# The last block of frames: scaled into DRAM, loaded in quarters, and turned by VectorE

## The chip, the cores and the metric

The kernel runs on one core of a Trainium2 chip. The metric is the device time of one execution in microseconds (us). Before the change the median of three runs is 937.81 us (937.69 to 938.49).

## The reference

One layer of a streaming encoder, in fp32, for 2048 prompt frames and 32 sample frames of 1024 columns:

- `hn = rmsnorm(h) * g_mix`, then one projection `hn @ w_in` to six parts of 512 columns (hA, bA, cA, zA, vB, zB).
- Mixer A: `u = cA * hA`, a causal convolution of width 3 over the frames, `yA = bA * conv * silu(zA)`. Mixer B: trailing means over 2, 4, 8 or 16 frames minus the frame, a 128x128 map per group of columns, `yB = that * silu(zB)`.
- `h += concat(yA, yB) @ w_out`, then `h += (p @ w_ple) * sigmoid(rmsnorm(h) @ w_gate)`, and a last rmsnorm.

The change concerns the first line alone: `hn` for the last 416 frames, and how its columns get onto the partitions, where the projection needs them.

## The kernel before, in words

The 2080 frames are five blocks of 416 (`NB`), in groups [0, 1], [2, 3] and [4]. A product is done in three passes of a rounded high part and the rest (`split`, lines 76 to 79: ACT casts, DVE subtracts). For a group of two blocks, seven products of halves replace eight, with sums of frames and of weights as operands.

The projection goes by units: four per group (j = 0 to 3), each with six kinds of weights for 128 columns. A unit of the first or second group runs three pairs of kinds (`pair`, line 847): seven products of halves a pair, and a `yield` between them. After each of these 24 steps of a unit `aside()` is called (line 949), which advances preparation of later frames: `at_pace(steps, num, den)` runs `num` steps of a generator per `den` calls. In the second group, from j = 1 on, the generator is `last_block` (line 1043), one step per three calls (line 1101).

`last_block` prepares block 4: three chunks of 128 prompt frames and one of 32 sample frames, c = 0 to 3. Per chunk, x is loaded (frames on partitions), ACT takes the sum of squares (line 88), POOL the scale factor (lines 69 and 73), DVE scales it by that and by g_mix (`normal`, line 406). Then in two halves of 512 columns: four 128x128 transposes on PE into PSUM (`turn`, line 413, against `ident`), and `to_memory` (line 480), which splits from PSUM into a staged tile and stores it to the DRAM tensor `b_d` from POOL's queue. The chunk takes three steps: scaling, half, half.

The third group frees the ring of frames (`xin`, five buffers of 128x1024 floats, which also holds the staged tiles), reads `b_d` into `hn[4]` (line 1077), and puts a pool `ya` into the freed memory, whose first loads (y, x and rows of w_out, lines 314, 327, 319) are issued as soon as it is free. A unit of this group is six plain products of 24 matmuls. After the projection come the products with w_out, the embedding, and the gate, whose frames are partly turned on PE (`turned`) and partly by loads in quarters and DVE's 32x32 blocks (`turned_here`, line 1297).

The order on each engine is set by a list scheduler: it orders what is ready by its own estimate of times, earlier traced first. `keep_in_program_order(ins)` pins an instruction behind the one traced before it on its engine (later ones may still be put ahead); every engine and every DMA queue then runs in that order. SP's queue carries the raw weights (line 511), the frames (line 392) and the stores of y_d (line 705).

Of the kernel before, what the change touches and what calls it, by code (L numbers as in the profile page):

```python
# [9 lines left out]
F32 = mybir.dt.float32  # L10
F32R = mybir.dt.float32r
AF = mybir.ActivationFunctionType
ALU = mybir.AluOpType
PSUM = bass.MemoryType.PSUM

P = 128
D = 1024
KC = D // P
# [6 lines left out]
NB = 416  # L25
# [3 lines left out]
KH = KC // 2  # L29
# [5 lines left out]
def trunk(ctx, tc, x_p, x_s, c_conv, c_pool, p_p, p_s, g_mix, w_in, conv_w, conv_b, pool_w,  # L35
          pool_scale, w_out, g_ple, w_gate, w_ple, g_fin, y_p, y_s, sc_p, sp_p, sc_s, sp_s):
    nc = tc.nc
# [38 lines left out]
    def split(hi, lo, src, eng=nc.vector):  # L76
        ins = nc.scalar.copy(hi, src)  # L77
        eng.tensor_tensor(lo, src, hi.bitcast(F32), op=ALU.subtract)
        return ins
# [3 lines left out]
    g_bc = const.tile([P, D], F32, name="g_bc")  # L83
# [20 lines left out]
    def embed(todo, wp, ring, queue=nc.sync):  # L104

        got = {}

        def prep(c):
            if c in got or c >= len(todo):
                return
            i = todo[c]
            r, n = tiles[i]
            if c % 4 == 0:
                pt = ring("p", i)
                m = min(4, len(todo) - c)
                full = [j for j in todo[c:c + m] if j < NT - 1]
                if full:  # L120
                    nc.sync.dma_start(pt.rearrange("p (a d) -> p a d", a=4)[:, :len(full)],
                                      p_p[r:r + len(full) * P].rearrange("(a p) d -> p a d", p=P))
                if len(full) < m:
                    nc.sync.dma_start(pt[:DEC, len(full) * PLE:(len(full) + 1) * PLE], p_s)
                got["p"] = pt
            pt = got["p"][:, (c % 4) * PLE:(c % 4 + 1) * PLE]
            pps = ring("pps", i)
            ptp = tbank(f"ptp_{i}")
            for k in range(2):
                nc.tensor.transpose(ptp[:, k * P:k * P + n], pt[:n, k * P:(k + 1) * P], ident[:n, :n])  # L130
            v = ptp.rearrange("p (k t) -> p k t", k=4)[:, :2, :n]
            split(pps[:, 0, :, :n], pps[:, 1, :, :n], v)
            got[c] = pps

        def run(c, last=False):
            i = todo[c]
            r, n = tiles[i]
            prep(c)
            prep(c + 1)
            prep(c + 2)  # L140
            pps = got[c]
            o = ring("out", i)
            for nh in range(2):
                cs = slice(nh * NH, nh * NH + NH)
                ps = bank(f"e_{i}_{nh}")
                embed_product(ps, pps, wp, cs, n)
                (nc.vector.tensor_copy if last and nh else nc.scalar.copy)(o[:n, cs], ps[:n])
            (nc.gpsimd if last else queue).dma_start(e_d[r:r + n], o[:n])

        return prep, run  # L150
# [141 lines left out]
    def slot(name):  # L292
        return acts[0].tile([P, SLOT], F32R, tag="hn", name=name)
# [13 lines left out]
    def ring4(t, name):  # L307
        return t.tile([P, D], F32, tag="t", name=name)
# [15 lines left out]
    def load_rows(pool, name, i, pr, sa=None):  # L324
        r, n = tiles[i]
        t = ring4(pool, f"{name}_{i}")
        nc.sync.dma_start(t[:n], pr[r:r + n] if sa is None else rows_of(pr, sa, r, n))
        return t

    with ExitStack() as s1:  # L330
# [5 lines left out]
        xin = frames_in.enter_context(tc.tile_pool(name="xin", bufs=5, side="right"))  # L336
# [11 lines left out]
        def put(piece, src):  # L348

            return split(piece[:, :, 0], piece[:, :, 1], src)  # L350
# [45 lines left out]
        def x_stat(x, later=False):  # L396

            t, n, name = x
            return t, n, sumsq(t, n, name, later=later)
# [4 lines left out]
        def normal(x):  # L404
            xt, n, r = x
            nc.vector.scalar_tensor_tensor(xt[:n], xt[:n], r[:n], g_bc[:n], op0=ALU.mult, op1=ALU.mult)  # L406

        def turn(x, half, name, get=tbank, later=False):
            xt, n, _ = x
            pt = get(name)  # L410
            for k in range(KH):
                kk = half * KH + k
                ins = nc.tensor.transpose(pt[:, k * P:k * P + n], xt[:n, kk * P:(kk + 1) * P], ident[:n, :n])
                if later:
                    tc.keep_in_program_order(ins)
            return pt.rearrange("p (k t) -> p k t", k=KH)[:, :, :n]
# [58 lines left out]
        b_d = tc.dram_tile([P, KC, 2, NB], F32, name="b_d")  # L475

        def staged(name):
            return xin.tile([P, KH, 2, P], F32R, tag="t", name=name)

        def to_memory(mem, name, src, at, n, t=None, later=False):  # L480
            t = t or staged(name)[:, :, :, :n]
            ins = put(t, src)
            if later:
                tc.keep_in_program_order(ins)
            nc.gpsimd.dma_start(mem[:, :, :, at:at + n], t.bitcast(F32))
# [98 lines left out]
        for c, x in enumerate([*ahead0, short0]):  # L584
            normal(x)
            n = P if c < 3 else DEC
# [433 lines left out]
        def load_ahead(g, c):  # L1020
            ahead[g, c] = columns_in(g, c) if g == 1 else [x_load(f"4_{c}", [x_rows(4, c)])]
# [21 lines left out]
        def last_block():  # L1043

            load_ahead(2, 0)
            for c in range(4):
                x = x_stat(ahead.pop((2, c))[0], True)
                if c < 3:
                    load_ahead(2, c + 1)
                normal(x)  # L1050
                yield
                for half in range(2):
                    pt = turn(x, half, f"pt4_{c}_{half}", later=True)
                    to_memory(b_d[:, half * KH:half * KH + KH], f"b_4_{c}_{half}", pt, c * P, x[1])
                    yield

        def at_pace(steps, num, den):

# [11 lines left out]
        for gi, tbs in enumerate(GROUPS):  # L1070
            if gi == 2:

                frames_in.close()
                t = slot("hn_4")
# [13 lines left out]
            for j in range(4):  # L1088
                unit = gi * 4 + j
                u = Unit(gi, tbs, j)  # L1090
                if unit == 0:
                    u.plain()
                    B0["T4"] = piece_of(seventh("B0_T4"), 0)
                    nc.sync.dma_start(B0["T4"].bitcast(F32), p_d["T4"])
                    p_d["T4"] = tc.dram_tile([P, KH, 2, NB], F32, name="p_dT4b")
                    aside = at_pace(next_columns(3, 0, 1, 2), 39, 62)
                elif gi == 0:
                    u.seven(B, aside)
                elif gi == 1:
                    if j == 1:  # L1100
                        aside = at_pace(last_block(), 1, 3)
                    u.seven(B, aside, j == 0)
                else:
                    u.plain()
                if gi == 2:
                    early_sums(j)
# [5 lines left out]
    with ExitStack() as s2:  # L1112
# [111 lines left out]
        for i in range(0, NT - 1, 2):  # L1224
            with tc.issue_after(loaded[-1].ins):
                x = [load_rows(xh, "x", i + b, x_p) for b in range(2)] if i else [first_x, second_x]
# [4 lines left out]
            if last:  # L1231
                n = tiles[NT - 1][1]
# [6 lines left out]
            if last:  # L1239
                x = load_rows(xh, "x", NT - 1, x_p, x_s)  # L1240
# [27 lines left out]
        _, run = embed(rest_e, wp, ring)  # L1268
# [195 lines left out]
        n = tiles[NT - 1][1]  # L1464
# [5 lines left out]
        h, e = (load_rows(*a) for a in ((xh, "h", NT - 1, h_d), (ya, "e", NT - 1, e_d)))  # L1470
        plain("gl", A, W, n, *short_ops(h, e, n))
        done_g(NT - 1, h)
        for i in range(0, NT - 3, 2):
            A = S.pop(i)
            h = [load_rows(xh, "h", i + b, h_d) for b in range(2)]
# [34 lines left out]
```

## Time and profile before

| | before |
|---|---|
| median of three runs | 937.81 us |
| the profiled execution | 940.76 us, its span 939.0 us |
| TensorE (PE) busy | 918.3 us, 98% |
| PE's weight loads busy | 829.4 us, 88% |
| VectorE (DVE) busy | 727.4 us, 77% |
| ScalarE (ACT) busy | 482.2 us, 51% |
| GpSimd (POOL) busy | 129.3 us, 14% |
| granted TensorE clock, mean | 0.992 |
| DMA | 182.97 MB, 195 GB/s |

The span runs from the first to the last instruction of the profiled execution; the 1.76 us around it are in its time. A group of instructions is shown with its line, engine, operation and its tiles, out<-in; "<-" behind an idle time names what ended it. Matmuls overlap one another in the records, so their cost is read from one start to the next. Numbers of tiles are left out in part, so tiles of several units share a name.

### The profile page before, as it was taken

How to read it: one execution, taken by the hardware profiler on the slowest of the kernel's cores; microseconds unless marked ns; L12 is line 12 of the kernel's file. 1: busy time of each engine (PE TensorE's matmuls, PEld its weight loads, DVE VectorE, ACT ScalarE, POOL GpSimd, SP SyncE). 2: the span in 40 equal slices, each digit the busy share in tenths (PEclk: the TensorE clock that was granted, in tenths of full speed). 3: DMA queues.
4: the chain of work that ended last, by engine and by line, in shares of the span. 5: the costliest groups of instructions: out<-in, count | busy, mean ns of one | idle time of the engine just before them, and what ended most of it. 6: DMA issues, size and time to landing. Idle time of an engine off the chain costs nothing.

```text
span 939.0 us, 13008 instructions
## 1 busy us (share of the span) xinstructions
PE 918.3 (98%) x4567; PEld 829.4 (88%) x4567; DVE 727.4 (77%) x1230; ACT 482.2 (51%) x894; POOL 129.3 (14%) x244
## 2 busy tenths in 40 slices
PE   6999999999999999999999999999999999999996
PEld 5899998999999999999999987888877868888885
DVE  6796898899588978685777589665554797888985
ACT  5653555464445554443444456334334875555663
POOL 2110232212000110000000010111211001211123
PEclk8999999999999999999999999999999999999998
DMA  8335556769955645427655359866785884566553
GB/s 240 85 121 175 154 146 203 222 174 297 417 167 139 180 142 166 129 71 272 195 167 175 128 187 289 270 181 183 218 244 171 318 264 129 206 220 244 183 207 113
DMA packets 133215, 182.97 MB, mean 195 GB/s; under 512 B 11164, under 2 KB 105116, under 8 KB 131869
## 3 DMA queue, kind: packets, MB, share of 16 engines
q1 hardware_dynamic: 117165, 131.70, 45.0%
q0 software_dynamic: 13248, 44.93, 14.6%
q10 hardware_dynamic: 2736, 5.51, 1.8%
q8 instruction: 36, 0.59, 0.3%
q14 instruction: 30, 0.25, 0.1%
HBM read 127.23 MB, written 54.86 MB: 194 GB/s over the span
## 4 chain that ended last, share of the span: by engine, by line
PE 79%; ACT 1%; DMA 1%; DVE 1%; POOL 0%; issue 0%; POOLq 0%; SPq 0%; ACTq 0%
PE x_o L167 9%; PE x_g L167 9%; PE x_zab L561 5%; PE x_ch L561 5%; PE x_zbv L561 5%; PE e L102 5%; PE z_g L167 5%; PE z_o L167 4%; PE z_ch L561 3%; PE z_zab L561 3%; PE z_zbv L561 2%; PE y_g L167 2%; PE y_o L167 2%; PE b L561 2%; PE za L561 2%; PE c L561 2%
## 5 line engine op out<-in xcount | busy, mean ns | idle before, releaser
L77 ACT CAST y_S<-y_fS 128x512 fp32r<-128x512 f32 x32 | 19.5, 621 | 43.1 <-PE x_o L167 19.4
L102 PE MATMUL e<-wq,pps 128*128 128x512 f32 (+1 forms) x156 | 38.8, 399 | 0.2 <-ACT pps L77 0.2
L406 DVE SCALAR_TENSOR_TENSOR xt<-xt,rstd_x,g_bc 128x1024 f32<-128x1024 f32 (+2 forms) x18 | 23.1, 1282 | 17.7 <-POOL rstd_x L73 17.5
L167 PE MATMUL x_g<-wg_b,g_S 128*128 128x512 f32 x128 | 35.9, 390 | 0.0
L167 PE MATMUL x_o<-wo_b,y_S 128*128 128x512 f32 x128 | 35.8, 391 | 0.0
L561 PE MATMUL x_zab<-B,w_zab_S 128*128 128x416 f32 x168 | 34.3, 352 | 0.5 <-ACT V L859 0.5
L561 PE MATMUL x_ch<-B,w_ch_S 128*128 128x416 f32 x168 | 34.6, 352 | 0.0
L561 PE MATMUL x_zbv<-B,w_zbv_S 128*128 128x416 f32 x168 | 34.4, 353 | 0.0
L561 PE MATMUL z_ch<-B,w_ch_S 128*128 128x416 f32 x168 | 34.1, 351 | 0.0
L561 PE MATMUL z_zbv<-B,w_zbv_S 128*128 128x416 f32 x168 | 34.1, 351 | 0.0
L561 PE MATMUL z_zab<-B,w_zab_S 128*128 128x416 f32 x168 | 34.0, 351 | 0.0
L102 PEld LDWEIGHTS e<-wq,pps 128*128 128x128 f32 (+1 forms) x156 | 27.4, 182 | 6.9 <-ACT pps L77 0.5
L561 PEld LDWEIGHTS x_zab<-B,w_zab_S 128*128 128x128 f32 x168 | 31.3, 188 | 1.1 <-ACT V L859 0.8
L561 PEld LDWEIGHTS x_zbv<-B,w_zbv_S 128*128 128x128 f32 x168 | 31.1, 188 | 0.8 <-ACT zs L859 0.4
L561 PEld LDWEIGHTS x_ch<-B,w_ch_S 128*128 128x128 f32 x168 | 31.2, 188 | 0.6 <-ACT c_s L859 0.3
L561 PEld LDWEIGHTS z_zab<-B,w_zab_S 128*128 128x128 f32 x168 | 31.4, 188 | 0.3
L561 PEld LDWEIGHTS z_ch<-B,w_ch_S 128*128 128x128 f32 x168 | 31.3, 188 | 0.4
L561 PEld LDWEIGHTS z_zbv<-B,w_zbv_S 128*128 128x128 f32 x168 | 31.3, 188 | 0.3
L69 POOL TENSOR_SCALAR ms_f<-ssq_f 128x1 f32<-128x1 f32 (+1 forms) x15 | 8.8, 588 | 160.7 <-ACT junk L88 160.7
L77 ACT CAST y<-y 128x512 fp32r<-128x512 f32 x24 | 14.8, 618 | 29.6 <-PE x_o L167 13.7
L1332 DVE SCALAR_TENSOR_TENSOR h<-h,rstd_f,g_bc 128x1024 f32<-128x1024 f32 (+1 forms) x15 | 19.3, 1284 | 12.7 <-POOL rstd_f L73 12.7
L167 PEld LDWEIGHTS x_o<-wo_b,y_S 128*128 128x128 f32 x128 | 24.0, 188 | 5.1 <-ACT c_o L1136 0.3
(571 smaller groups left out, 2670.4 us busy)
## 6 DMA issues: line engine op xcount, KB each, us to landing
y<-y_d SPq DMA_DIRECT2D x16, 512.0 KB, 12.8
x<-in_x_prompt_dram SPq DMA_DIRECT2D x16, 512.0 KB, 9.0
h_d<-x SPq DMA_DIRECT2D x16, 512.0 KB, 4.8
h<-h_d SPq DMA_DIRECT2D x16, 512.0 KB, 4.1
xt<-in_x_prompt_dram SPq DMA_DIRECT2D x15, 512.0 KB, 6.4
e<-e_d SPq DMA_DIRECT2D x15, 512.0 KB, 6.3
out_dram<-h POOLq DMA_DIRECT2D x14, 512.0 KB, 3.0
p_dT<-T POOLq DMA_DIRECT2D x12, 512.0 KB, 5.4
```

The costliest lines, as they stand in the source:

```text
L69: nc.gpsimd.tensor_scalar(ms[:n], ssq[:n], scalar1=1.0 / D, scalar2=EPS, op0=ALU.mult, op1=ALU.add)
L77: ins = nc.scalar.copy(hi, src)
L102: nc.tensor.matmul(ps[:n], pps[:, a, k, :n], wp[k][b][:, cs], start=k + q == 0, stop=k == 1 and q == 2)
L167: nc.tensor.matmul(ps[:n], lhs[:, k, a, :n], w[b][:, k], start=start and k + q == 0, stop=k == KH - 1 and q == 2, skip_group_check=True)
L406: nc.vector.scalar_tensor_tensor(xt[:n], xt[:n], r[:n], g_bc[:n], op0=ALU.mult, op1=ALU.mult)
L561: nc.tensor.matmul(ps[:, :NB], lhs[:, k, x], b[:, k, y], start=start and k + q == 0, stop=stop and k == KH - 1 and q == 2, skip_group_chec ...
L1332: nc.vector.scalar_tensor_tensor(h[:n], h[:n], rf[:n], g_bc[:n], op0=ALU.mult, op1=ALU.mult)
```

## The change

`last_block` no longer turns the chunks on PE.

- Scaling (`scaled_to_memory`): DVE scales in four pieces of 256 columns. Piece q takes from each of the eight runs of 128 columns (k) the 32 columns q*32 to q*32+31, and writes them side by side, in another tile of the ring `xin`. POOL's queue stores the tile to a new DRAM tensor `xs_d`. The pieces are pinned in DVE's order.
- Loading (`from_memory`): SP's queue loads quarter q of `xs_d` onto partitions 32q to 32q+31, with the chunk's groups of 32 frames beside each other.
- Turning (`turned_in_place`): one DVE instruction turns every 32x32 block in place, pinned in DVE's order. That leaves column on the partition and frame along it, as the transposes did.
- `halves_to_memory` splits the halves from SBUF and stores them to `b_d` as before. The ACT cast is pinned, as it was.

The generator has 18 steps where it had 12. Chunk c is scaled in one step, the chunk before it is turned, split and stored in the next two, and then chunk c is loaded; the first chunk is loaded in the step after its scaling. The pace stays at a step per three calls.

```diff
             load_ahead(2, 0)
-            for c in range(4):
+            back = {}
+
+            def scale(c):
                 x = x_stat(ahead.pop((2, c))[0], True)
                 if c < 3:
                     load_ahead(2, c + 1)
-                normal(x)
+                scaled_to_memory(x, c * P)
+                return x[1]
+
+            def halves_to_memory(c, n):
+                u = turned_in_place(back.pop(c))
+                for half in range(2):
+                    t = staged(f"b_4_{c}_{half}")[:, :, :, :n]
+                    v = lambda h: t[:, :, h].rearrange("p k (g t) -> p k g t", t=32)
+                    tc.keep_in_program_order(split(v(0), v(1), u[:, half * KH:half * KH + KH]))
+                    nc.gpsimd.dma_start(b_d[:, half * KH:half * KH + KH, :, c * P:c * P + n], t.bitcast(F32))
+                    yield
+
+            for c in range(5):
+                n = scale(c) if c < 4 else 0
                 yield
-                for half in range(2):
-                    pt = turn(x, half, f"pt4_{c}_{half}", later=True)
-                    to_memory(b_d[:, half * KH:half * KH + KH], f"b_4_{c}_{half}", pt, c * P, x[1])
-                    yield
+                if c:
+                    yield from halves_to_memory(c - 1, m)
+                if n:
+                    back[c], m = from_memory(c * P, n), n
+                yield
+
+        xs_d = tc.dram_tile([NB, D], F32, name="xs_d")
+
+        def scaled_to_memory(x, r):
+
+            xt, n, rs = x
+            t = ring4(xin, f"xs_{r}")
+            v = lambda a, q: a[:n].rearrange("p (k q c) -> p q k c", q=4, c=32)[:, q]
+            for q in range(4):
+                o = t[:n, q * 256:q * 256 + 256].rearrange("p (k c) -> p k c", c=32)
+                tc.keep_in_program_order(nc.vector.scalar_tensor_tensor(o, v(xt, q), rs[:n], v(g_bc, q),
+                                                                        op0=ALU.mult, op1=ALU.mult))
+            nc.gpsimd.dma_start(xs_d[r:r + n], t[:n])
+
+        def from_memory(r, n):
+
+            t = ring4(xin, f"xb_{r}")[:, :n * KC]
+            for q in range(4):
+                nc.sync.dma_start(t[q * 32:q * 32 + 32].rearrange("p (g c) -> p g c", c=256),
+                                  xs_d[r:r + n, q * 256:q * 256 + 256].rearrange("(g p) c -> p g c", p=32))
+            return t
+
+        def turned_in_place(t):
+
+            tc.keep_in_program_order(nc.vector.transpose(t, t))
+            return t.rearrange("p (g k t) -> p k g t", k=KC, t=32)
```

## The prediction

> **What bounds the kernel now.** I read first the page's table of slices, then the busy time by stretch, then PE in order of time where the last block is turned, and last the waits of VectorE (DVE), SyncE's queue (SP) and GpSimd's queue (POOL). The page, slices of 23.5 us:
>
> ```profile
> PE   6999999999999999999999999999999999999996
> DVE  6796898899588978685777589665554797888985
> ```
>
> The stretches below are: the last unit of the first group; units j=1, 2, 3 of the second group, where the last block's generator runs; the third group; and the products after it. The columns after the width are PE, PE's weight loads, DVE, ACT, POOL (busy us, instructions), the granted clock, DMA share, GB/s.
>
> ```profile
> 185.00:237.00 52.00, 51.96 (x282) 50.88 (x281) 50.48 (x87) 27.74 (x51) 11.42 (x17) 1.00 0.74 232
> 288.00:340.00 52.00, 52.00 (x284) 50.97 (x283) 44.01 (x70) 27.72 (x50) 7.49 (x12) 1.00 0.47 136
> 340.00:392.00 52.00, 52.00 (x281) 50.82 (x280) 41.79 (x72) 23.12 (x42) 3.61 (x4) 1.00 0.60 177
> 392.00:437.00 45.00, 45.00 (x240) 44.54 (x239) 33.53 (x52) 19.52 (x34) 1.12 (x2) 1.00 0.44 149
> 437.00:549.00 112.00, 112.00 (x598) 110.30 (x598) 79.88 (x183) 51.26 (x102) 8.07 (x16) 1.00 0.53 160
> 549.00:725.00 176.00, 175.19 (x767) 139.84 (x766) 111.79 (x176) 78.92 (x138) 27.02 (x51) 1.00 0.74 226
> 760.00:930.00 170.00, 170.00 (x783) 138.96 (x782) 146.07 (x213) 100.05 (x174) 29.38 (x50) 1.00 0.57 196
> ```
>
> PE never idles from 288 to 549 and loses 0.8 us in the 176 after that, at the full clock: whatever is taken off PE's queue here moves the rest forward, as long as nothing else becomes late. The first row shows the cover: DVE busy for 50.48 of 52 us, and PE still loses 0.04.
>
> PE around four of the eight groups of transposes (start, us, then the group; x12 is one product of a half):
>
> ```profile
> 342.54 0.60 PE L413 MATMUL pt<-ident,xt 128*128 128x128 f32 x4
> 342.90 2.51 PE L561 MATMUL x_zbv<-B,w_zbv_S 128*128 128x416 f32 x12
> 345.25 2.43 PE L561 MATMUL z_zbv<-B,w_zbv_S 128*128 128x416 f32 x12
> 347.51 2.43 PE L561 MATMUL x_zbv<-B,w_zbv_S 128*128 128x416 f32 x12
> ...
> 352.05 2.43 PE L561 MATMUL x_zbv<-B_T,w_zbv 128*128 128x416 f32 x12
> 354.41 0.43 PE L413 MATMUL pt<-ident,xt 32*128 32x32 f32 x4
> 354.77 2.53 PE L561 MATMUL x_ch<-B,w_ch 128*128 128x416 f32 x12
> 357.13 2.43 PE L561 MATMUL y_ch<-B,w_ch 128*128 128x416 f32 x12
> ```
>
> An undisturbed product takes 347.51 - 345.25 = 2.26 us from start to start. Four full transposes hold the queue for 0.36 us, and the product behind them takes 2.35, 0.09 more: 0.45. Around the short four it is 0.10 + 0.36 + 0.10 = 0.56. The printed 0.60 is no price, as instructions overlap.
>
> **The change part by part.** *Removed from PE:* all transposes of the generator, by the row
>
> ```profile
> L413 PE MATMUL pt<-ident,xt x32: 220/272/273, 298.2 to 362.0; 128*128 128x128 f32 x24, 32*128 32x32 f32 x8
> ```
>
> that is six full groups and two short: 6 x 0.45 + 2 x 0.56 = **3.82 us off PE**. The Trainium skill, "VectorE: DVE Perf Modes", The three transpose paths, puts a 128x128 turn on TensorE at 390 ns and says that VectorE turns 32x32 blocks only, which it calls useless for some layouts; its rules send a 128x128 turn to TensorE. By 390 ns each, 24 turns would be 9.4 us and the time about 928.4, an estimate from that page for 2-byte data; here the rows above give 0.45 for four, so the trace does not bear it out.
>
> *Added to DVE:* the turns, and the scaling in four pieces. From the gate stage, and from this generator:
>
> ```profile
> L1304 DVE STREAM_TRANSPOSE hn<-hn x8: 1235/1236/1247, 760.2 to 900.1; 128x1024 f32<-128x1024 f32 x8
> ```
> ```profile
> L78 DVE TENSOR_TENSOR b<-pt,b x8: 281/676/684, 299.6 to 362.6; 128x512 fp32r<-128x512 f32 x6, 128x128 fp32r<-128x128 f32 x2
> ```
> ```profile
> 295.01 1.28 DVE L406 SCALAR_TENSOR_TENSOR xt<-xt,rstd_x,g_bc 128x1024 f32<-128x1024 f32 x1 [0.73 <-POOL rstd_x L73]
> 313.09 1.28 DVE L406 SCALAR_TENSOR_TENSOR xt<-xt,rstd_x,g_bc 128x1024 f32<-128x1024 f32 x1 [1.14 <-POOL rstd_x L73]
> ```
>
> Three turns of 1.24 and one of 256 columns (between 0 and 1.24; I take a quarter, 0.31): 4.0 us. For the pieces, 128 columns cost 0.28 and 512 cost 0.68, so some 0.15 is fixed per instruction. Three more per chunk cost between nothing (starts overlap) and 0.45, over four chunks up to 1.8; I take 1.8, the safe side. A piece's view in runs of 32 does not occur for this instruction; the bounds are 1.28 in all, and twice that (4 x 1.28 more); I take no penalty, since the gate stage reads such views as fast as dense ones. Its sums and ACT casts from turned frames, against the generator's cast from PSUM:
>
> ```profile
> L1437 DVE TENSOR_TENSOR g_fS<-hn x8: 669/691/694, 762.8 to 901.4; 128x512 f32<-128x512 f32 x8
> ...
> L77 ACT CAST g<-hn x8: 614/617/621, 769.8 to 908.1; 128x512 fp32r<-128x512 f32 x8
> L78 DVE TENSOR_TENSOR g<-hn,g x8: 673/682/684, 771.2 to 909.2; 128x512 fp32r<-128x512 f32 x8
> ```
> ```profile
> L77 ACT CAST b<-pt x8: 272/580/589, 298.9 to 362.3; 128x512 fp32r<-128x512 f32 x6, 128x128 fp32r<-128x128 f32 x2
> ```
>
> So a subtraction is 0.68 from PSUM or SBUF, and a cast 0.04 longer: eight of them are 0.3 us on an ACT that is half idle. **DVE gets 5.8 us**, with the bounds 3.7 and 11.9.
>
> Does PE feel it? The generator grows from 12 to 18 steps, one per three calls; the first transposes (step 1, call 6) start at 298.2 and the last (step 11, call 36) at 361.9, so a call is 2.13 us and a step 6.4. The work spreads over 2.1 units instead of 1.5. In the first unit DVE loses four scalings and five subtractions (5.1 + 3.4) and gets three scalings, two turns, three subtractions (5.2 + 2.5 + 2.0): 44.0 + 1.2 = 45.2. In the second it gets one scaling, 1.55 of turns, four subtractions of which one is short: 41.8 - 1.3 + 5.6 = 46.1. Both are under the 50.48 that hid, so I cost this at nothing; without that cover its price would be the 5.8.
>
> *Added to the queues:* four stores of up to 512 KB on POOL, and 16 loads on SP, by quarters. Longest waits of SP from 280 to 440 that concern this, and what POOL's stores (line 485) and the gate stage's quarter loads (line 1302) take to land, each with its issue row:
>
> ```profile
> SPq L1079 <- DVE xt L406: 12.9, 1, 12.9
> ...
> SPq L314 <- DMA b_d<-b: 8.0, 2, 5.8
> ```
> ```profile
> L485 POOL DMA_DIRECT2D b_d<-b x8: 885/894/983, 300.6 to 363.2; - x8
> ...
> DMA to landing us min/median/max: 3.1/4.8/6.7
> ```
> ```profile
> L1302 SPq DMA_DIRECT2D hn<-h_d x29: 318/432/1464, 755.1 to 892.3; - x29
> ...
> DMA to landing us min/median/max: 2.5/3.0/10.6
> ```
>
> About 3.4 MB more move in 110 us, some 31 GB/s on top of 136 to 177, where 232 moved in the first row above. On POOL a store waits for its scaling, with the next chunk's scale factor behind it, which that scaling precedes by two steps. The waits on the way back matter more: a load waits at the head of SP for its store, with the next raw weights queued behind; the turn is pinned in order on DVE, with weight halves and PSUM sums behind it. For the first chunk the scaling ends at 296.3, and its turn belongs to step 3, where the second chunk's scaling stands now, at 313.1: 16.8 us are there. Medians need 0.89 + 4.8 + 4 x 0.43 + 3.0 = 10.4, so 6.4 are spare. Later chunks have five steps, 32 us. So I cost the round trip at nothing. The waits for the scale factor stay as they are:
>
> ```profile
> DVE xt L406 <- POOL rstd_x L73: 5.0, 3, 3.1
> ```
>
> DVE stood for 3.1 us once and PE lost nothing in that unit: that is the longest DVE stall shown harmless here.
>
> *Moved:* the store of the last piece of b_d goes from call 36 to call 51, about 394; with issue and landing it ends by 402. The block itself is read back from 426.1 on, so 24 us remain. The loads of the next stage that need the same memory move with it, from 366 to some 402.
>
> **The sum.** The profiled run took 940.76 us: a span of 939.0 and 1.76 around it; the median is 937.81, 2.95 lower. 940.76 - 3.82 = 936.9 for a run like that; taken off the median, **934.0**. The likeliest case has its own range, 933.2 (the 0.8 us that PE loses later go too) to 935.9.
>
> **The rivals.** *Late turn, gain eaten.* With the longest figures the first round trip takes 0.98 + 6.7 + 4 x 1.46 + 10.6 = 24.1 us, 7.3 late; over 3.1 shown harmless, PE loses 4.2: 934.0 + 4.2 = 938.2. For it: the maxima occurred, and DVE is busy for 85% here. Against: all at once, and the median leaves 6.4 us.
>
> *Slower: SP held.* SP stood for 12.9 us on one load that waited for a scaling. If it stands so ahead of a chunk's quarters and the load lands as late as the latest, the first turn comes after 0.89 + 4.8 + 12.9 + 1.7 + 10.6 = 30.9 us, 14.1 late; DVE holds the weight halves behind it, and PE loses 11.0: **945.0**. It decides from a turn that is 3.1 + 3.8 + 1.9 = 8.8 us late. For it: SP's queue waits in order, and that wait happened in this stretch. Against: it happened at the last chunk's scaling, and later chunks have 32 us.
>
> *Slower: the third group's first block.* Its two loads:
>
> ```profile
> L1077 POOL DMA_DIRECT2D hn<-b_d x2: 548/559/570, 426.1 to 426.7; - x2
> ...
> DMA to landing us min/median/max: 7.0/8.8/10.7
> ```
> ```profile
> L561 PEld LDWEIGHTS zb<-hn,w_zb x17: 187/188/188, 436.8 to 439.9; 128*128 128x128 f32 x17
> ```
>
> The second half lands at 437.4 at the latest and is wanted one product after 436.8, at 439.1: 1.7 us of slack. The displaced loads
>
> ```profile
> 366.51 0.92 SPq L314 DMA_DIRECT2D y<-y_d  x2
> 367.47 0.50 SPq L327 DMA_DIRECT2D x<-in_x_prompt_dram  x1
> ...
> 375.42 1.30 SPq L319 DMA_DIRECT2D wo_q<-in_w_out_dram  x2
> ```
>
> went out within 9 us, so if they fall on 426 they make it up to 9 late: 934.0 + (9 - 1.7) = 941.3. Against: 402 plus 10 is 412.
>
> *The transposes were free.* If PE only waits elsewhere for what it saves, 937.8; against it stand the rows without any idle PE. I count it with the first rival.
>
> **How the numbers follow.** Forecast 0.60; late turn or saving lost 0.17; SP held 0.14; third group's block 0.07; below 933.2 the last 0.02. A measurement of this kernel can tell about 0.2% (1.9 us) from no change: faster is under 935.9, slower over 939.7. So faster 0.62, same 0.17, slower 0.21. The range 933.2 to 941.3 leaves out the held SP and the 0.02, 0.16; DVE at its upper bound of 11.9 us falls into it with the first rival.
>
> **What would show it.** Right: no instruction of line 413 after 288, PE still full in the three units, the third group's first product 3.8 us earlier than 436.8, and the end with it; DVE at 45 and 46 of 52; the turns about 1.24 us with little idle ahead of them. Wrong: idle PE between 310 and 400 put down to weight halves or to a turn that waits for its load; SP waiting for xs_d by more than 6 us with raw weights behind; quarter loads landing over 10 us; scalings above 0.43 per piece; or PE full but for a first product of the third group that waits for its block.

## The result, and the profile after

The changed kernel takes 934.47 us (median of 13 runs, 932.9 to 938.18), the kernel before 938.08 us (median of 13). The ratio is 0.9966 with the 95% interval 0.9954 to 0.9978: 3.2 us less, between 2.1 and 4.3. Faster was forecast, at 934.0.

The page of the changed kernel, whose slices are 23.4 us wide:

```profile
span 934.1 us, 12992 instructions
...
PE 914.4 (98%) x4535; PEld 825.0 (88%) x4535; DVE 730.9 (78%) x1246; ACT 482.2 (52%) x894; POOL 129.0 (14%) x248
...
PE   7999999999999999999999999999999999999996
...
DVE  6896898899488989785677679655554798888985
```

PE is busy 3.9 us less than in the kernel before and still 98% of a shorter span; DVE has 3.5 us more. Next the busy time by stretch: two units in which the last block is turned, then the third group and the products behind it.

```profile
288.00:340.00 52.00, 51.70 (x274) 50.84 (x274) 46.41 (x81) 27.38 (x49) 7.06 (x12) 1.00 0.63 179
340.00:392.00 52.00, 52.00 (x277) 51.48 (x276) 44.81 (x76) 25.52 (x47) 6.23 (x8) 1.00 0.50 150
...
433.50:545.50 112.00, 112.00 (x597) 110.04 (x596) 80.23 (x181) 52.72 (x106) 8.02 (x16) 1.00 0.52 156
```

PE is as full as before, but for 0.30 us in the first of them. The third group's first product is the last row of this view of PE in order of time, first the changed kernel and then the kernel before:

```profile
428.89 2.43 PE L561 MATMUL x_zab<-B_T,w_zab 128*128 128x416 f32 x12
431.16 4.70 PE L561 MATMUL zb<-hn,w_zb 128*128 128x416 f32 x24
```
```profile
434.74 2.43 PE L561 MATMUL x_zab<-B_T,w_zab 128*128 128x416 f32 x12
437.01 3.19 PE L561 MATMUL zb<-hn,w_zb 128*128 128x416 f32 x16
```

It starts 5.85 us earlier, which is more than was taken away. So a start must be chosen that the change can't touch. I take the last x_zab product of the second group's unit j = 0, just ahead of the generator (286.64 before, 284.24 after), and cut the span there, at the third group's first product, at the embedding's first product (e) and at the gate's first product (x_g). All experiments below are read by this table (us, from one start to the next):

| | start to j = 0's end | the stage | third group, w_out | embedding | gate to the span's end |
|---|---|---|---|---|---|
| before | 286.64 | 150.37 | 283.94 | 47.60 | 170.45 |
| after | 284.24 | 146.92 | 284.15 | 48.39 | 170.40 |
| difference | -2.40 | -3.45 | +0.21 | +0.79 | -0.05 |

**The first 2.40 us are chance.** In the profile before, the granted clock was half for 10.2 us in two stretches near the start, in the one after never there. Rows by stretch, before and then after (the clock is the third number from the end):

```profile
15.00:22.00 7.00, 6.13 (x23) 5.82 (x24) 7.00 (x13) 4.37 (x10) 0.00 (x0) 0.51 0.75 252
39.00:42.50 3.50, 3.50 (x11) 3.32 (x12) 3.32 (x7) 2.40 (x7) 0.00 (x0) 0.51 0.18 63
```
```profile
15.00:22.00 7.00, 6.78 (x31) 6.47 (x32) 6.53 (x14) 4.55 (x10) 0.00 (x0) 1.00 0.86 295
```

The same code shows it or not: in ten other profiles, of kernels whose text is the same up to that place, the start to j = 0's end took 282.20 to 288.01 (284.71 in e2, the changed kernel again, and 288.01 in e9). A stretch of 3.4 us costs up to 1.7, where PE has work all through it, and the mean clock of the single runs (0.991 to 0.998) goes with their spread of 5 us. **The change is in the columns behind it:** 3.45 us won in the stage, and 0.79 given back in the embedding. (The 0.21 of the third column is within what equal code scatters there: 283.69 to 284.30, and 284.76 in e8.) The experiments ask where the missing 0.37 of 3.82 went, what covers DVE's new work, and where the 0.79 comes from.

### The profile page after: what moved, and what is told of

It is laid out like the page before. It is cut to its first block, busy times and chain, and to the rows that moved or that the text cites. A ratio compares the mean times of both kernels' runs of the same rounds, so it can differ in the third digit from the quotient of the medians.

```text
span 934.1 us, 12992 instructions
## 1 busy us (share of the span) xinstructions
PE 914.4 (98%) x4535; PEld 825.0 (88%) x4535; DVE 730.9 (78%) x1246; ACT 482.2 (52%) x894; POOL 129.0 (14%) x248
## 4 chain that ended last, share of the span: by engine, by line
PE 69%; DMA 5%; DVE 4%; ACT 2%; issue 1%; POOL 0%; POOLq 0%; SPq 0%; ACTq 0%; DVEq 0%
PE x_g L167 9%; PE x_o L167 8%; PE x_ch L561 5%; PE x_zbv L561 5%; PE x_zab L561 5%; PE z_g L167 5%; PE z_o L167 4%; PE z_ch L561 3%; PE z_zbv L561 2%; DMA wg_r<-g_d 2%; PE z_zab L561 2%; PE y_g L167 2%; PE y_o L167 2%; PE b L561 2%; PE za L561 2%; PE c L561 2%
## 5 line engine op out<-in xcount | busy, mean ns | idle before, releaser
L69 POOL TENSOR_SCALAR ms_x<-ssq_x 128x1 f32<-128x1 f32 (+2 forms) x18 | 8.7, 484 | 152.0 <-ACT junk L88 151.9
```

The source lines that it names most:

```text
L69: nc.gpsimd.tensor_scalar(ms[:n], ssq[:n], scalar1=1.0 / D, scalar2=EPS, op0=ALU.mult, op1=ALU.add)
```

## The experiments

The ratio is to the kernel before, with its interval, from runs on the same chip. Line numbers are those of each kernel.

| | median us | ratio | interval | the stage | embedding |
|---|---|---|---|---|---|
| e1 no turns at all | 935.48 | 0.9966 | 0.9952 to 0.9980 | 146.54 | 48.31 |
| e2 changed kernel again | 934.78 | 0.9965 | 0.9953 to 0.9977 | 146.92 | 48.01 |
| e3 changed, and transposes | 936.38 | 0.9982 | 0.9971 to 0.9994 | 149.81 | 47.60 |
| e10 turned three times | 935.87 | 0.9971 | 0.9958 to 0.9984 | 147.25 | 47.65 |
| e4 turned five times | 943.57 | 1.0059 | 1.0047 to 1.0071 | 155.70 | 47.65 |
| e5 loads from POOL's queue | 934.56 | 0.9951 | 0.9938 to 0.9964 | 146.92 | 47.99 |
| e7 scale factors a step earlier | 939.00 | 1.0003 | 0.9991 to 1.0016 | 150.96 | 47.95 |
| e9 the same, short chunk as it was | 934.59 | 0.9961 | 0.9945 to 0.9978 | 146.36 | 47.66 |
| e11 e9 and e5 together | 934.46 | 0.9965 | 0.9948 to 0.9983 | 146.36 | 47.72 |
| e8 64 PE instructions at the start | 938.89 | 1.0004 | 0.9995 to 1.0013 | 146.92 | 47.61 |
| e6 gate's frames turned too | 963.93 | 1.0265 | 1.0251 to 1.0278 | 146.92 | 49.14 |

### e1, e2, e3: is it the transposes?

e1 is the kernel before with its last block not turned at all, and with ACT's cast pinned as the changed kernel has it (the kernel before pins the transposes there, and not the cast); e2 the changed kernel again; e3 the changed kernel with the eight groups of transposes put back ahead of each chunk's scaling, from unscaled frames, unread. The edits of e1 and e3:

```diff
-                    pt = turn(x, half, f"pt4_{c}_{half}", later=True)
-                    to_memory(b_d[:, half * KH:half * KH + KH], f"b_4_{c}_{half}", pt, c * P, x[1])
+                    src = x[0] if c < 3 else g_bc
+                    pt = src[:, half * NH:half * NH + KH * x[1]].rearrange("p (k t) -> p k t", k=KH)
+                    to_memory(b_d[:, half * KH:half * KH + KH], f"b_4_{c}_{half}", pt, c * P, x[1], later=True)
```
```diff
+                for half in range(2):
+                    turn(x, half, f"pt4_{c}_{half}", later=True)
```

> The kernel before with the last block's 32 transposes left out and nothing put in their place: the halves are split straight from the scaled frames (for the short chunk from the g_mix rows), so the last block is not turned and the third group's results are not the reference's. Theory (the gain is PE's queue time, all that is added is hidden): 3.8 us below the kernel before, ratio 0.9959, and so the same as the changed kernel within its interval; PE's third-group start 3.8 us earlier relative to the point before the first group of transposes. Rival (the additions cost something that the gain pays for): clearly faster than the changed kernel, by 1 us or more. Rival (the transposes were no cost, and the gain is a side effect of another order): 938, ratio 1.0.

> The changed kernel again, on the same chip as the other three, as their yardstick. Theory: ratio 0.996 to 0.997; along PE's order, eight steps of some 0.45 us at the places of the eight groups of transposes. Rival (the earlier profile's 2.4 us at the start belong to the change): PE is again 2.4 us ahead by 200 us.

> The changed kernel with the eight groups of transposes put back on PE, from the unscaled frames into PSUM, where nothing reads them. Everything that the change adds is there, and PE saves nothing. Theory: 3.8 us above the changed kernel, so the time of the kernel before, 938, ratio 0.999 to 1.001. Rival (the additions cost PE something): above the kernel before by that, ratio over 1.001. Rival (the gain is not PE's time): stays at 934 to 935.

The stage of e2 is that of the changed kernel to the digit. Without any turning it is 150.37 - 146.54 = 3.83 us shorter: the price of 3.82, worked out from starts, is shown. The changed kernel gets 0.38 less than that. e3 gives most of it back: its stage is 2.89 longer than the changed kernel's. It is not the whole 3.82, since the scheduler put its transposes in rows of eight. PE of e3:

```profile
299.71 2.43 PE L561 MATMUL x_zbv<-B_T,w_zbv 128*128 128x416 f32 x12
301.99 1.03 PE L413 MATMUL pt<-ident,xt 128*128 128x128 f32 x8
302.78 2.51 PE L561 MATMUL x_ch<-B,w_ch 128*128 128x416 f32 x12
305.13 2.43 PE L561 MATMUL y_ch<-B,w_ch 128*128 128x416 f32 x12
```

302.78 - 301.99 = 0.79, and the product behind takes 2.35, 0.09 over 2.26: 0.88 for eight, where two fours took 0.90. The four such rows sum to 3.43. The other half microsecond is what the changed kernel's one PE wait costs, told below. e3 lacks it, though DVE stands there for 3.1 us as well: a row of eight transposes comes just ahead (328.93), and PE wants its next tile 0.88 us later. So the mechanism holds from both sides. By time alone e3's interval still lies under 1; the stage's starts tell what the time can't.

### e10 and e4: how much can DVE still take?

The turn in place is repeated; an odd count leaves the same result. The edit of e4 (e10 has 3 in place of 5):

```diff
-            tc.keep_in_program_order(nc.vector.transpose(t, t))
+            for _ in range(5):
+                tc.keep_in_program_order(nc.vector.transpose(t, t))
```

> The changed kernel with each VectorE turn done three times: 8.3 us more on VectorE, about 5 of them in the unit of j=1, 46.4 + 5.0 = 51.4 of 52 us, and 44.8 + 3.4 = 48.2 in the next. Theory (free time of a unit is the cover): no more than 0.5 us above the changed kernel, ratio 0.996 to 0.9975. Rival (what counts is the length of one block on VectorE's queue, as 4.5 us cost PE 3.1): the block of a turn with its scaling behind it, 3 x 1.2 + 1.6 = 5.2 us, costs PE 1 to 3 us, ratio over 0.998.

> The changed kernel with each VectorE turn done five times in place (an odd number gives the same block): 4 x 1.24 us more on VectorE for each of three chunks and 4 x 0.44 for the short one, 16.6 us in all, two of the large ones in the unit of j=1, where VectorE is busy for 46.4 of 52 us. Theory (the cover is VectorE's free time in a unit): 46.4 + 9.9 = 56.3 exceeds 52, so PE loses about 4 us in the first unit and less in the second (44.8 + 6.7 = 51.5), and the time is 937 to 940. Rival (PE's lead in weights is deep enough for any stall of this size): 934 to 935, no change.

e10 adds 2 x (3 x 1.24 + 0.44) = 8.3 us to DVE, and the stage grows by 0.33. Its rival is not tested by that: the scheduler put other instructions between the repeated turns (306.80, 309.50 and 311.24 for the first chunk), so no block of 5.2 us stood on DVE. e4 adds 16.6, and the stage grows by 8.78. By stretch in e4:

```profile
288.00:340.00 52.00, 51.71 (x274) 50.72 (x273) 47.66 (x78) 23.61 (x43) 6.16 (x11) 1.00 0.57 169
340.00:392.00 52.00, 46.94 (x231) 44.41 (x230) 50.37 (x80) 24.37 (x44) 4.92 (x7) 0.93 0.46 129
```

DVE is at 97% in the second unit, and PE has lost 5 us of busy time and 7% of its clock. Most of both is one event, in PE's order of time and by stretch (the other waits there are 0.8, 0.5 and 0.4 us):

```profile
364.87 3.83 PE L561 MATMUL z_ch<-B,w_ch_S 128*128 128x416 f32 x10 [3.40 <-DVE w_ch_S L78]
```
```profile
362.50:369.50 7.00, 4.63 (x13) 4.42 (x14) 7.00 (x13) 1.64 (x3) 2.42 (x3) 0.52 0.53 166
```

DVE never pauses there, the weight half w_ch_S comes 3.4 us late, and around that wait the clock is halved from 362.8 to 369.6, in which PE's products take about twice as long: of the 4.7 us that it works there, 2.4 are lost. I had expected 937 to 940, since I had reckoned DVE's overflow, and no clock. The cover is real, and its edge lies between 8 and 17 us more DVE work.

### e5: do the loads hold SP?

The sixteen quarter loads are issued from POOL's queue instead.

```diff
-                nc.sync.dma_start(t[q * 32:q * 32 + 32].rearrange("p (g c) -> p g c", c=256),
+                nc.gpsimd.dma_start(t[q * 32:q * 32 + 32].rearrange("p (g c) -> p g c", c=256),
```

> The changed kernel with the 16 quarter loads on POOL's queue in place of SP's, where they had held SP for 23.3 us in three waits. Theory (SP's holds cost nothing, as raw weights land early enough): the changed kernel's time within its interval, ratio 0.9955 to 0.9975. Rival (the holds cost part of the gain): 0.5 us or more below the changed kernel. Rival (POOL's queue now holds the scale factors and stores): PE idle at line 862 or a scaling over 3 us late, and slower than the changed kernel.

What SP's queue waited for in the changed kernel from 280 to 440 (total, times, longest, us):

```profile
SPq L1090 <- DMA xs_d<-xs: 23.3, 3, 9.8
...
SPq L314 <- DMA b_d<-b: 8.1, 1, 8.1
SPq L1121 <- DVE xs L1082: 8.1, 1, 8.1
```

The hold of the rival is there, with 23.3 us in sum. In e5 no load of quarters is on SP any more:

```profile
SPq L511 <- DVE w_ch_S L78: 22.8, 3, 11.5
...
SPq L392 <- DMA xs_d<-xs: 9.8, 1, 9.8
```

One load of frames still stands behind a store whose tile it takes, and the raw weights (line 511) now wait longer for their own buffers, which DVE frees (for w_ch_S 9.5 us in the changed kernel). The ratio, 0.9951, is a little below the range that the theory gave, but the stage is 146.92 us to the digit, as in the changed kernel. So the hold is real and costs nothing here: the weights queued behind it could not have gone out much sooner.

### e7, e9, e11: the 0.3 us, and a wait that cost 3 us

In the changed kernel PE waits once from 280 to 440. DVE stood for the third chunk's scale factor, did the pinned pieces, and only then came to U, which frees the PSUM tile of the next product. DVE and PE of the changed kernel:

```profile
329.10 1.67 DVE L1082 SCALAR_TENSOR_TENSOR xs<-xt,rstd_x,g_bc 128x256 f32<-128x256 f32 x4 [2.76 <-POOL rstd_x L73]
330.69 0.59 DVE L862 TENSOR_TENSOR U<-x_zab,U 128x416 f32<-128x416 f32 x1
```
```profile
328.61 2.43 PE L561 MATMUL z_zab<-B,w_zab_S 128*128 128x416 f32 x12
331.33 2.53 PE L561 MATMUL x_zab<-B_T,w_zab 128*128 128x416 f32 x12 [0.29 <-DVE U L862]
```

2.76 + 1.67 = 4.4 us in which DVE does nothing for PE. That length alone isn't the cause. The kernel before has 4.4 us at the same place; its DVE and PE:

```profile
333.33 1.28 DVE L406 SCALAR_TENSOR_TENSOR xt<-xt,rstd_x,g_bc 128x1024 f32<-128x1024 f32 x1 [3.09 <-POOL rstd_x L73]
```
```profile
332.83 2.43 PE L561 MATMUL z_zab<-B,w_zab_S 128*128 128x416 f32 x12
335.17 2.54 PE L561 MATMUL x_zab<-B_T,w_zab 128*128 128x416 f32 x12
337.55 0.60 PE L413 MATMUL pt<-ident,xt 128*128 128x128 f32 x4
```

In both the factor comes 1.8 us before x_zab could follow z_zab at 2.26. With one scaling of 1.28 the two products take 2.34 and 2.38 from start to start, 0.19 too long together; with the pieces, 0.39 longer, it is 2.72 and 2.37, 0.57 too long. The difference, 0.38, is all that the stage lacks of e1's 3.83. e10 agrees: there DVE, busy with turns, stands for 1.00 us only, and PE waits 0.30 as well. e7 takes each factor one step earlier, behind the loads of the chunk before; e9 does so for the prompt chunks alone (c < 2 in the last test, and stat(3) at the head of scale(3)); e11 is e9 with e5's edit. The edit of e7:

```diff
+            stats = {}
+            def stat(c):
+                stats[c] = x_stat(ahead.pop((2, c))[0], True)
+            stat(0)
             def scale(c):
-                x = x_stat(ahead.pop((2, c))[0], True)
+                x = stats.pop(c)
...
                     back[c], m = from_memory(c * P, n), n
+                    if c < 3:
+                        stat(c + 1)
```

> The changed kernel with each later chunk's sum of squares and scale factor one step before its scaling. VectorE waited 4.2 us for factors at the head of its queue, and PE 0.3 us behind it. Theory (that 0.3 us is the pinned scaling's price): the waits for the factor and PE's 0.3 us at line 862 go, the time falls by 0.3, which the timing can't tell from none. Rival (the 0.3 us is the turns' load on VectorE): PE's wait stays.

> The kernel with the factors a step earlier, but the short chunk's factor again in the step of its scaling. In that kernel VectorE stood 4.5 us at the short chunk's scaling, which the scheduler had put 20 VectorE instructions earlier, and PE lost 3.1 us behind it and 1.7 to a halved clock. Theory (the loss is that one pinned scaling, waiting for a buffer of the ring whose store had not landed): both go, and with them the 0.3 us at the third chunk's scaling: 934 to 935, ratio 0.995 to 0.997. Rival (earlier factors of any chunk make VectorE late): stays at 938 to 939.

> The kernel with the factors of the second and third chunk a step earlier, and the quarter loads on POOL's queue as well: both edits that take a wait off a busy queue. Theory: 0.3 us below the changed kernel, within what the timing can tell, ratio 0.995 to 0.997; PE idle nowhere between 288 and 430. Rival (POOL's queue then holds a factor behind a load): a DVE wait for a factor over 3 us and a PE wait behind it, slower than the changed kernel.

e7 failed: DVE's waits for factors shrink from 4.2 to 1.5 us in all and PE's 0.3 us is gone, but the stage is 4.04 us longer. The list scheduler now put the short chunk's scaling, ready early, 20 DVE instructions further ahead; there it had no free tile. DVE, PE and the granted clock in e7:

```profile
340.70 0.68 DVE L78 TENSOR_TENSOR b<-xb,b 128x512 fp32r<-128x512 f32 x1
345.85 1.66 DVE L1091 SCALAR_TENSOR_TENSOR xs<-xt,rstd_x,g_bc 32x256 f32<-32x256 f32 x4 [4.47 <-issue]
...
349.36 0.58 DVE L862 TENSOR_TENSOR V<-x_zbv,V 128x416 f32<-128x416 f32 x1
```
```profile
350.00 3.31 PE L561 MATMUL x_zbv<-B_T,w_zbv 128*128 128x416 f32 x11 [2.78 <-DVE V L862]
```
```profile
351.00:354.50 3.50, 3.50 (x13) 3.32 (x12) 2.72 (x5) 1.36 (x3) 0.00 (x0) 0.51 0.00 1
```

DVE stands for 4.47 us, PE for 2.78, and PE then runs 3.4 us at half clock, another 1.7. Against e9's stage the loss is 4.60, and 2.78 + 1.7 = 4.5. What DVE waits for is not named. The time fits a store of b_d from a tile of the ring `xin`, where the scaling needs one: it was issued at 337.60 and took 8.2 us to land, which is 345.8, and the scaling starts at 345.85. No run separates that store from other causes. That the pinned scaling of the short chunk is the culprit is shown: e9 leaves it where it was, and neither PE nor its weight loads wait for anything from 280 to 440. The stage of e9 and e11 is 146.36, 0.56 under the changed kernel, and 0.18 under e1, which has the shorter wait of the kernel before. The time can't tell that from it: the intervals of e9, e11, e5 and the changed kernel overlap, so none is called better.

The Trainium skill, "TensorE: Matmul & The Clock Gate", Part 1, says that the clock halves after an idle window of about 3.4 us, one that runs free of the program. The lengths agree: 3.4 us in e7, 6.8 in e4. The idle time doesn't: 2.78 us was enough in e7, and the clock was still 1.00 there from 350.5 to 351.0, when PE had been at work again for a microsecond.

### e8: what takes time back in the embedding?

In the embedding the changed kernel loses 0.79. PE's one added wait there (0.4 us) is for ACT, which had stood for weights of the gate. ACT before, and then after:

```profile
739.39 0.62 ACT L77 CAST wg_c<-wg_r 128x512 fp32r<-128x512 f32 x1 [1.03 <-DMA wg_r<-g_d]
```
```profile
735.28 0.62 ACT L77 CAST wg_c<-wg_r 128x512 fp32r<-128x512 f32 x1 [2.50 <-DMA wg_r<-g_d]
```

From e's first product that is 18.44 us before and 19.97 after. The load was issued 4.19 us ahead of its cast before, 5.67 after. The DMA queues of the changed kernel while it was under way show something that the kernel before doesn't have there:

```profile
q8 instruction: 1, 0.02, 1.0%
```

That is 16 KB of instructions for an engine. It comes 17.9 us after the last matmul on w_out began; before, it came after 10.5, ahead of the load. Taking instructions from PE would move the points at which its next ones are fetched: PE has 4567 matmuls before and 4535 after, each with its weight load. In e3, again with 4567, it comes after 11.3 us and the embedding takes 47.60; in e1, e2, e5 and e7 it comes after 17.3 to 17.8, and the embedding takes 47.95 to 48.31. e8 puts as many back, where they have no other use: 32 small transposes at the start, into a PSUM tile that nobody reads.

```diff
+    pad = tbank("pad")
+    for _ in range(32):
+        nc.tensor.transpose(pad[:32, :32], ident[:32, :32], ident[:32, :32])
```

> The changed kernel with 32 transposes of 32x32 of the identity first in PE's order, while PE waits for frames, and unread: 64 more PE instructions, as many as the change removed. Along PE's order the changed kernel lost 0.9 us at the gate stage's start, where the kernel before lost nothing: its fourth load of gate rows landed 1.5 us later, together with a 16 KB fetch of instructions that came 7 us earlier in the kernel before. Theory (the place of that fetch is set by the count of PE instructions before it): the fetch is back at 10 to 11 us after the last product with T4, and the gate stage's PE waits go; 0.9 us below the changed kernel. Rival (PE's earlier arrival, or chance, makes those waits): they stay as in the changed kernel.

The fetch is back at 10.5 us, and the embedding at 47.61, as before. ACT of e8:

```profile
740.21 0.62 ACT L80 CAST wg_c<-wg_r 128x512 fp32r<-128x512 f32 x1 [0.26 <-DMA wg_r<-g_d]
```

The total doesn't tell, and the 0.9 us that were forecast did not come: e8 is 4.3 us slower than e5 by the medians (same chip, 938.89 and 934.56). Its profile reaches the end of j = 0 at 290.84, 6.6 us later than the changed kernel's, with 10.2 us at half clock, and its third group and w_out take 0.6 more; whether the transposes at the start cause that was not tried.

Nor does the late fetch cost by itself. In e4, e9, e10 and e11 it comes late (17.5 to 17.8 us) as well, e10 has 2.40 us of the wait shown above, and the embedding takes 47.65 to 47.72 there. What decides is a later load. ACT's last cast into wg_c, before and then after:

```profile
756.10 0.62 ACT L77 CAST wg_c<-wg_r 128x512 fp32r<-128x512 f32 x1 [0.50 <-DMA wg_r<-g_d]
```
```profile
752.90 0.62 ACT L77 CAST wg_c<-wg_r 128x512 fp32r<-128x512 f32 x1 [1.49 <-DMA wg_r<-g_d]
```

In the five kernels that lose 0.35 to 0.79 (the changed one, e1, e2, e5 and e7) it starts 37.15 to 37.59 us after e's first product, and the gate's first product comes 10.80 us behind it, to 0.01. So they lose just what it is later than 36.80. In the other kernels of the table, e6 apart, it starts by 36.74 and they lose at most 0.12. From the issue of its load to the cast it is 4.83 to 5.18 us in the five and 3.95 to 4.34 in the others. No fetch is beside this load in the five; before, e3 and e8 have one there and lose nothing. The late fetch, and the wait beside it, can at most use up spare time; why the last load takes longer in the five stays open. That the fetch is PE's is inferred from the counts, since the profile doesn't say.

### e6: does the same pay in the gate stage?

There half of the frames are still turned on PE. e6 turns them with quarter loads and DVE too.

```diff
...
+                upper.extend(turned_here(i))
...
-                a11, a12 = turned(i)
+                a11, a12 = upper
...
```

> The changed kernel with the same trade in the gate stage: the even frames too are loaded in quarters and turned by VectorE, which removes 16 groups of four transposes from PE and 16 casts from ACT there, and adds eight turns of 1.24 us to a VectorE that is busy for 146.5 of 170 us. Theory (a group is worth 0.45 us as long as VectorE has free time): 16 x 0.45 = 7.2 us below the changed kernel, ratio about 0.989. Rival (at 92% VectorE no longer covers, or the chain from load to turn to sums starts the stage later): less than half of it, or slower.

It is 2.65% slower, as the rival had it. What PE's weight loads waited for from 740 on, the busy time in one of the four periods, and SP's waits:

```profile
PEld x_g L167 <- ACT g L77: 23.6, 5, 7.3
```
```profile
822.00:868.00 46.00, 40.88 (x168) 32.85 (x167) 36.56 (x52) 21.08 (x36) 6.51 (x11) 0.93 0.57 178
```
```profile
SPq L327 <- DMA out_dram<-h: 59.7, 10, 8.1
```

DVE is at 80%, less than the 89% that hid in the second group, so its busy share isn't what runs out. In this period SP stands for 6.7 us behind such a store, the next pair's load is issued after it, at 823.2, and landed by 828.1; its turn, behind sums on DVE, comes at 831.74, and PE stands for 5.12 us until 833.70, again with the clock halved (833.0 to 839.8). SP's wait alone is no explanation, since the changed kernel has it too (63.3 us in all). There half of the frames need no turn on DVE; here the chain from load to turn to cast stands ahead of a pair's first product, and PE's weight loads wait for that cast five times. What would loosen it, more tiles to work ahead or another order, wasn't tried.

## Why the prediction was right, and where its terms were off

- **PE's price of the transposes, 3.82.** Right: 3.83 in e1, which keeps the other waits of the kernel before. It came from starts, and the groups' printed durations would have given 6 x 0.60 + 2 x 0.43 = 4.5.
- **DVE hides the turns.** Right, with spare (the pieces are not hidden everywhere, see the scale factor below): DVE forecast 45.2 and 46.1 of 52, measured 46.41 and 44.81; that is 5.4 more than before in the two together, of 5.8 forecast. e10 shows 8 us more almost free, e4 that 17 more cost 8.8. The single prices, by groups of the changed kernel from 288 to 415:

```profile
L1082 DVE SCALAR_TENSOR_TENSOR xs<-xt,rstd_x,g_bc 128x256 f32<-128x256 f32 x12 | 5.0, 479 | 3.5 <-POOL rstd_x L73 3.5
...
L1096 DVE STREAM_TRANSPOSE xb<-xb 128x1024 f32<-128x1024 f32 x3 | 3.7, 1238 | 0.0
...
L1096 DVE STREAM_TRANSPOSE xb<-xb 128x256 f32<-128x256 f32 x1 | 0.4, 435 | 0.0
```

  Pieces of 256 in runs of 32 take 0.479 one by one and 1.64 to 1.67 by four, where 1.73 was reckoned and up to 2.56 bounded: views in short runs cost nothing extra. The short turn took 0.44, not 0.31: with 1.24 for four times the columns, some 0.17 of it is fixed.
- **The round trip is free.** Right, and faster than the medians used. The stores land in 3.0 us where 4.8 was taken, the quarters in 3.6 where 3.0 was. The first chunk was stored at 294.57, its loads went out from 297.72, and it was turned at 306.60, sooner than the 313.1 that the pace suggested (310.7, when the 2.4 us of the start are taken off), without idle time ahead of it:

```profile
306.60 1.24 DVE L1096 STREAM_TRANSPOSE xb<-xb 128x1024 f32<-128x1024 f32 x1
307.76 1.64 DVE L1082 SCALAR_TENSOR_TENSOR xs<-xt,rstd_x,g_bc 128x256 f32<-128x256 f32 x4
```

- **SP held.** The wait was real, 9.8 us at the longest, over the 6 that I named as a sign of trouble; the sign was badly chosen. Only what is due behind a wait makes it cost. e5 shows that nothing was.
- **The third group's first block.** Its slack held: the last store of b_d went out at 389.80, earlier than 394 (391.6 without the 2.4), and the third group starts without a wait.
- **The waits for the scale factor stay.** This step was off by 0.4. That 3.1 us of idle DVE cost PE nothing was a misreading: PE shows no idle time in that unit, but its weight loads wait 0.3 us for U there, and two products take 0.19 us longer. So nothing was spare at that place, and the three added instructions, 0.39 of the 0.45 per chunk that the prediction reckoned for DVE and held to be hidden, came out of PE's time: 0.38. e9 has both back, 0.56.
- **The rest moves forward unchanged.** The step that failed most, and the smallest to see: 0.79 us went in the embedding, where the prediction put the loss at nothing, or hoped for 0.8 more. What shows in its place is the last load of gate weights landing up to 0.8 us past the point where ACT's cast of it holds up the gate; equal code lost between 0.05 and 0.79 there, and why the load lands late is not settled.
- **The sum.** 3.45 - 0.79 = 2.7 in the one profile, 3.2 (2.1 to 4.3) by the runs, 3.82 forecast: the mechanism was right, and the gain somewhat smaller than the sum had it. That the two profiled runs lie 4.9 us apart (940.76 and 935.86) is luck for half of it, the 2.40 of the start.

## What to carry to other kernels

Where one engine is full for hundreds of microseconds, work moved off it is worth what its queue loses from start to start (here 3.82 reckoned and 3.83 measured); read that from the starts, and then search the receiving engine for pinned instructions that stand ahead of what the full engine needs, not for its busy share. A wait at the head of a queue is harmless or dear by what is due behind it, and an instruction that is pinned and moved earlier can wait for a tile that isn't free, as e7 did. When a change of 0.3% is judged, cut the span at places that it can't touch, so that chance at the start of a run isn't taken for its effect. And before a wait is blamed, see whether the loss moves with it from run to run: the longest wait of ACT for weights in the embedding is there without a loss too.

## What the runs showed of the hardware that was not expected

- A pause of PE costs more than its length: after one of 2.78 us the granted clock fell to 0.51 for 3.4 us (e7), around 3.40 for 6.8 us (e4), around 5.12 for 6.8 us (e6). Half of what PE works in such a stretch is lost on top: 1.7 us in e7, 2.4 in e4.
- Eight transposes in a row held PE for 0.88 us, two groups of four for 0.90 by the rows quoted.
- Instructions are loaded in pieces of 16 KB by the same DMA engines as data (35 of them in the changed kernel). With 64 PE instructions fewer such a load came about 7 us later against the work, and with 64 put back (e8) where it had been; no price of that was found.
